# S5 states by two full-width sums and four transfers, gate banks read under priority, seven-product sums on VectorE, running column sum added last

## The chip, the cores and the metric

The kernel runs on one NeuronCore of a Trainium2 chip. Five engines work from queues of their own and wait for each other by semaphores: PE (TensorE, matmuls), DVE (VectorE), ACT (ScalarE), POOL (GpSimd) and SP (SyncE, which here only issues transfers). The time is the device time of one execution in microseconds, and lower is better. The time before is a median of 3 runs.

## The reference, cut to what matters

One inference step of a two-layer hybrid decoder over 1048 columns (16 meta tokens, 1024 prompt tokens, 8 sample tokens), all in float32. Layer 0 has a gated linear attention beside an S5 state space model; layer 1 is a Griffin block, a gelu branch times an RG-LRU recurrence; each layer ends with a gated feed-forward network.

```
# S5: a diagonal complex scan, then the output from the states
Ar, Ai, xr, xi = lax.associative_scan(_cplx_combine, (a_re, a_im, bu_re, bu_im), axis=1)
x0r = x0_re.astype(f32)[:, None]
x0i = x0_im.astype(f32)[:, None]
xr, xi = xr + Ar * x0r - Ai * x0i, xi + Ar * x0i + Ai * x0r
y = (jnp.einsum('ghp,btgp->btgh', c_re.astype(f32), xr)
     - jnp.einsum('ghp,btgp->btgh', c_im.astype(f32), xi)
     + d.astype(f32) * uf).reshape(B_, T, S5_W)
# rmsnorm, ahead of each mixer and each feed-forward network
y = xf * lax.rsqrt(jnp.mean(xf * xf, axis=-1, keepdims=True) + EPS)
```

## The kernel before

The model's width of 1024 lies on partitions in 8 tiles of 128, the columns on the free axis in chunks of 352, 352 and 344 (or 262 in layer 1). Every float32 product is three fp32r matmuls: an operand is split into a high part (`whi`, `H`, cast by ACT on line 85) and a low part (`wlo`, `L`, a subtraction on DVE), and `mm3` (lines 128 to 130) sums high times high, low times high and high times low in one PSUM bank. There are four such banks with the tag "bank" and four with the tag "aux", whose tiles are called `p`. A bank comes free when DVE or ACT has read it. The elementwise helpers `tt` (line 45) and `stt` (line 48) record most operations of DVE and POOL, so that tiles tell operations apart better than lines.

The stages by time in the trace: inputs to 60 us; the S5 states to 225; attention, GLU and output projection to 476; the rest of the output projection and the preparation of the first feed-forward to 541; feed-forward up to 968 and down to 1240; the RG-LRU layer to 1725; its last output projection and the preparation of the second feed-forward to 1784; feed-forward up to 2200 and down to the end.

**S5.** The 32 channel groups come in four states of 8. For one state, small tables are made on DVE, POOL and PE (`s5tm`, `s5CA`, `s5E`; PE transposes `s5E` on line 366), the inputs are projected (line 400), and `s5_states` rotates, scans (line 432) and rotates back, with `s5WC` and `s5WS` as the rotation, made by POOL. The parts of the rotation back are `s5ZA` and `s5VR`; their sum or difference is the state, `s5XP`, which is `[128, 8, 138]`: real and imaginary part on the two halves of the partitions, one column range for each group, while `s5ZA` and `s5VR` have two groups on the halves of the partitions. `s5XR` and `s5SO` are the small pieces for the sample columns and the output states. PE then forms the output by pairs, a matmul with `s5U` on line 465 and one with `s5XP` on line 466, and ACT evicts it. Between these pieces PE computes the products for K, Q and V.

**First feed-forward, preparation.** The feed-forward multiplies in a seven-product scheme (`Seven`). For each of four pairs of tiles, `Seven.sums` forms four differences `t` of gained halves, each then split to `T` by ACT and DVE. All this runs beside the output projection, whose banks DVE adds to the residual `X` under priority, and beside the running sum `acc` of squares on POOL.

**Griffin layer.** A step (half of the columns, group of three tiles) makes `rR` in xr, then the gelu branch in `gelu_branch` (six banks, each read by DVE as `rgg <- bank * RB`), then the recurrences on DVE (`rh`, `rig`, a scan on line 1540), the product of both (`rgg <- rgg * rh`, split to `ryh` and `ryl`), and the output projection. **After the last output projection** (`after`) come the squares for the norm: tiles 0 to 5 go into `acc` on POOL, which a matmul with ones (`colsum`, line 147) sums over the partitions into a bank `tot`; tiles 6 and 7 are summed straight into it.

The order on each engine is not written by hand. A scheduler takes the program's order, a model of readiness and the priorities given by `tc.high_priority()`, and fixes one order for each engine; waits come from the tiles that are shared.

Of the kernel before, what the change touches and what calls it, by code (L numbers as in the profile page):

```python
# [9 lines left out]
F32 = mybir.dt.float32  # L10
# [4 lines left out]
MUL, ADD, SUB = ALU.mult, ALU.add, ALU.subtract  # L15
# [24 lines left out]
def hybrid_step_kernel(ctx: ExitStack, tc: tile.TileContext, a: dict):  # L40
    nc = tc.nc
    V, A, P, PE = nc.vector, nc.scalar, nc.gpsimd, nc.tensor

    def tt(o, x, y, op, eng=None):
        return (eng or V).tensor_tensor(out=o, in0=x, in1=y, op=op)  # L45
# [13 lines left out]
    ps = ctx.enter_context(tc.tile_pool(name="ps", bufs=8, space=PSUM))  # L59
# [86 lines left out]
    def colsum(p, x, first=True, last=True):  # L146
        PE.matmul(out=p, lhsT=ones, rhs=x, start=first, stop=last)
# [25 lines left out]
    RB = qk.tile([128, T], F32, name="RB")  # L173
# [157 lines left out]
    NG, NI = 8, 4  # L331
# [50 lines left out]
    def s5_states(bi, d, tabs):  # L382
# [10 lines left out]
        VR = s5p.tile([128, 2, NI, 138], F32, name="s5VR")  # L393
        for j in range(0, NI, 2):
            m = 2
            for par in range(2):
                p = ps.tile([128, 2, 146], F32, name="p", tag="aux", bufs=4)
# [37 lines left out]
        XR = s5p.tile([128, 3, 2, NI, 8], F32, name="s5XR")  # L435
        nc.sync.dma_start(out=XR[:, 0], in_=a["s5xr"][:, :, sl])
        A1 = d["A1"]
        tt(XR[:, 1], XR[:, 0], A1[:, 0, sl].unsqueeze(1).unsqueeze(3).to_broadcast([128, 2, NI, 8]), MUL)
        tt(XR[:, 2, 0], XR[:, 0, 1], A1[:, 2, sl].unsqueeze(2).to_broadcast([128, NI, 8]), MUL)
        tt(XR[:, 2, 1], XR[:, 0, 0], A1[:, 1, sl].unsqueeze(2).to_broadcast([128, NI, 8]), MUL)  # L440
        tt(XR[:, 1], XR[:, 1], XR[:, 2], ADD)
        tt(SO[:, :, :, 0:8], XR[:, 1], VR[:, :, :, 0:8], ADD)
        tt(ZA, ZB, wc, MUL)
        tt(VC[:, 0], ZB[:, 1], WS, MUL)
        tt(VC[:, 1], ZB[:, 0], WS, MUL)
        XP = s5p.tile([128, NG, 138], F32, name="s5XP")
        P.memset(XP[:, :, 0:1], 0.0)
        nc.sync.dma_start(out=XP[:, :, 130:138], in_=a["s5xh"][:, g0:g0 + NG])
        for ri in range(2):
            for par in range(2):  # L450
                rows = slice(par * 64, par * 64 + 64)
                xo = XP[ri * 64:ri * 64 + 64].rearrange("p (i two) c -> p i two c", two=2)[:, :, par]
                tt(xo[:, :, 1:130], ZA[rows, ri, :, 0:129], VC[rows, ri, :, 0:129], ADD if ri else SUB)
            tt(SO[:, ri, :, 8], ZA[:, ri, :, 129], VC[:, ri, :, 129], ADD if ri else SUB)
        P.dma_start(out=a["o_s5"][:, :, sl], in_=SO)
        return U, XP

# [535 lines left out]
    class Seven(Stats):  # L993
# [18 lines left out]
        def sums(self, j, x1, x2, pool):  # L1012

            g1, g2 = (CV[:, self.gain + m:self.gain + m + 1] for m in (j, j + 4))
            b12, t1, t2 = (pool.tile([128, HALF], F32, name="t7", bufs=3) for _ in range(3))

            def gained(o, x, g):
                A.activation(out=o, in_=x, func=ACTF.Copy, scale=g)

            gained(t1, x1[:, :HALF], g1)  # L1020
            gained(b12, x1[:, HALF:], g1)
            tt(t1, b12, t1, SUB, P)
            gained(t2, x2[:, HALF:], g2)
            tt(b12, t2, b12, SUB, P)
            tt(t2, t2, t1, SUB, P)
            split(*self.o["T2", j], t2)
            split(*self.o["T3", j], b12)
            split(*self.o["T1", j], t1)
            gained(t1, x2[:, :HALF], g2)
            tt(t1, t1, t2, SUB, P)  # L1030
            split(*self.o["T4", j], t1)

        def gained(self, m, x):
# [521 lines left out]
    def gelu_branch(half, G, ws):  # L1555
        h0 = half * HALF
        ggs = []
        for w in ws:
            gg = rq.tile([128, HALF], F32, name="rgg", bufs=3)
            for c0, n in HCH:  # L1560
                p = bank()
                mm3(p[:, :n], kslices(w), cols(HL[half], c0, n))
                tt(gg[:, c0:c0 + n], p[:, :n], RB[:, h0 + c0:h0 + c0 + n], MUL)
            ggs.append(gg)
        return ggs

# [18 lines left out]
    def after(m, c0, n):  # L1585

        x = X[m][:, c0:c0 + n]
        if m in (0, 1, 4, 5):
            if m == 0:
                nxt.acc[c0] = tp.tile([128, 352], F32, name="acc", bufs=3)  # L1590
            sumsq_step(nxt.acc[c0], x, n, m == 0)
            if m == 5:
                tot[c0] = ps.tile([128, 512], F32, name="p", tag="aux", bufs=4)[:, :n]
                colsum(tot[c0], nxt.acc.pop(c0)[:, :n], last=False)
        else:

            q = tp.tile([128, 352], F32, name="sq", bufs=2)
            A.square(out=q[:, :n], in_=x)
            colsum(tot[c0], q[:, :n], first=False, last=m == 7)
            if m == 7:  # L1600
                A.activation(out=RB[:, c0:c0 + n], in_=tot[c0], func=ACTF.Sqrt, bias=eps, scale=1.0 / 1024)
                nxt.late.append((0, c0, n))
        if c0 + n == T:
            P.dma_start(out=xdn[m][:, HALF:], in_=X[m][:, HALF:])
            nxt.gained(m, X[m][:, HALF:])
            if m >= 4:
                g = nxt.sums_in(m - 4, X[m - 4], X[m])
                next(g)
                if m < 6:
                    next(g)  # L1610
                else:
                    rest.append(g)
# [196 lines left out]
```

## Time and profile before

| | |
|---|---|
| median of 3 runs | 2488.47 us (2487.82 to 2498.07) |
| profiled execution | 2490.02 us, of which the span is 2488.2 us |
| PE busy | 2372.1 us, 95% of the span |
| DVE busy | 1802.1 us, 72% |
| ACT, POOL busy | 1139.8 us, 589.9 us |
| mean granted TensorE clock | 0.978 of full speed |

The span runs from the first to the last instruction. PE is the engine to look at: what it does not fill of the span is idle, and a view of what ended each idle time names the engine that it waited for. The clock column (PEclk) is the share of the full 2.4 GHz that was granted; in this trace a stretch is either at 1.00 or at 0.50, so a mean between is a mix of both.

### The profile page before, as it was taken

The page shows a single profiled execution, that of the slowest core. Times are in us where ns is not written, and L with a number is a line of the kernel's source. Part 1 is how long each engine was busy: PE and PEld are TensorE (multiplying, and loading weights), DVE is VectorE, ACT ScalarE, POOL GpSimd, SP SyncE. Part 2 cuts the span into 40 slices and gives each one's busy share as a digit, 9 for nine tenths or more (in the row PEclk, how much of TensorE's full clock was granted, in tenths as well). Part 3 has the DMA queues.
Part 4 walks back from the last instruction along what each step waited for, and adds up shares of the span by engine and source line. Part 5 has one row for each costly group of instructions (what it writes and reads, how often), then busy time and mean ns, then how long its engine had stood idle before and what let it go on. Part 6 is the DMA issues. An engine that isn't in the chain of part 4 may idle for free.

```text
span 2488.2 us, 45222 instructions
## 1 busy us (share of the span) xinstructions
PE 2372.1 (95%) x17443; PEld 2326.2 (93%) x17443; DVE 1802.1 (72%) x3183; ACT 1139.8 (46%) x2302; POOL 589.9 (24%) x607
## 2 busy tenths in 40 slices
PE   6879999989999999999999999999799999999998
PEld 6768988879999999999999999998799999999997
DVE  9885788688777777554688777777877777766445
ACT  5224564554444444321576666665544444453123
POOL 4331000283443332000220002210333333310003
PEclk9999999989999999999999999999899999999999
DMA  3422225633333332632133333323333333336221
GB/s 117 108 70 80 87 71 168 212 128 122 118 116 116 116 116 94 211 109 89 43 90 94 99 99 122 93 89 100 128 116 116 116 116 116 116 119 195 90 82 70
DMA packets 200831, 277.09 MB, mean 111 GB/s; under 512 B 34440, under 2 KB 114264, under 8 KB 200616
## 3 DMA queue, kind: packets, MB, share of 16 engines
q1 hardware_dynamic: 191016, 261.94, 33.1%
q0 software_dynamic: 2848, 9.81, 1.0%
q10 hardware_dynamic: 6752, 2.45, 0.4%
q8 instruction: 137, 2.24, 0.4%
q14 instruction: 78, 0.64, 0.1%
HBM read 216.69 MB, written 51.43 MB: 108 GB/s over the span
## 4 chain that ended last, share of the span: by engine, by line
PE 74%; DVE 8%; issue 5%; DMA 3%; ACT 2%; POOL 1%; SPq 0%; DVEq 0%; POOLq 0%; ACTq 0%
PE bank L128 18%; PE bank L129 18%; PE bank L130 18%; PE p L128 6%; PE p L129 6%; PE p L130 6%; DVE X L45 1%; DVE wlo L45 1%; DVE rh L1540 1%; DMA hr<-hdr 1%; PE p L779 1%; DMA hr<-xdn 1%; DVE rig L48 0%; DMA SS<-in_st 0%; POOL acc L45 0%
## 5 line engine op out<-in xcount | busy, mean ns | idle before, releaser
L85 ACT CAST whi<-wraw 128x512 fp32r<-128x512 f32 (+2 forms) x449 | 262.1, 590 | 450.5 <-PE bank L129 328.0
L45 DVE TENSOR_TENSOR wlo<-wraw,whi 128x512 fp32r<-128x512 f32 (+2 forms) x448 | 327.9, 738 | 127.6 <-ACT whi L85 112.6
L45 DVE TENSOR_TENSOR X<-X,bank 128x352 f32<-128x352 f32 (+4 forms) x388 | 187.1, 486 | 194.8 <-PE bank L130 192.8
L128 PE MATMUL bank<-ph,whi 128*128 128x352 f32 (+1 forms) x912 | 293.1, 322 | 2.0 <-DVE X L45 1.8
L129 PE MATMUL bank<-pl,whi 128*128 128x352 f32 (+1 forms) x912 | 294.0, 322 | 0.0
L130 PE MATMUL bank<-ph,wlo 128*128 128x352 f32 (+1 forms) x912 | 293.7, 322 | 0.0
L45 POOL TENSOR_TENSOR acc<-acc,sq 128x352 f32<-128x352 f32 (+3 forms) x97 | 106.7, 1105 | 556.4 <-ACT sq L143 555.2
L85 ACT CAST whi<-wS 128x512 fp32r<-128x512 f32 x176 | 109.0, 620 | 262.2 <-PE p L129 127.1
L45 DVE TENSOR_TENSOR wlo<-wS,whi 128x512 fp32r<-128x512 f32 x176 | 125.2, 712 | 122.3 <-ACT whi L85 120.6
L128 PE MATMUL bank<-b,whi 128*128 128x262 f32 x560 | 164.2, 293 | 18.3 <-DVE rgg L45 9.8
L128 PE MATMUL bank<-H,whi 128*128 128x352 f32 (+1 forms) x480 | 161.4, 339 | 18.0 <-DVE X L45 8.1
L128 PEld LDWEIGHTS bank<-ph,whi 128*128 128x128 f32 x912 | 171.3, 188 | 3.2 <-DVE X L45 2.6
L129 PEld LDWEIGHTS bank<-pl,whi 128*128 128x128 f32 x912 | 171.3, 188 | 0.8
L130 PEld LDWEIGHTS bank<-ph,wlo 128*128 128x128 f32 x912 | 171.3, 188 | 0.0
L45 POOL TENSOR_TENSOR wS<-wA 128x512 f32<-128x512 f32 x88 | 151.5, 1721 | 69.5 <-DVE wlo L45 60.7
L129 PE MATMUL bank<-L,whi 128*128 128x352 f32 (+1 forms) x480 | 160.9, 337 | 7.0 <-DVE L L48 7.0
L130 PE MATMUL bank<-b,wlo 128*128 128x262 f32 x560 | 163.0, 291 | 3.9 <-DVE wlo L45 3.9
L129 PE MATMUL bank<-b,whi 128*128 128x262 f32 x560 | 163.1, 291 | 0.0
L128 PE MATMUL bank<-a,whi 128*128 128x262 f32 x560 | 160.5, 287 | 0.4 <-DVE rgg L45 0.4
L130 PE MATMUL bank<-H,wlo 128*128 128x352 f32 (+1 forms) x480 | 158.9, 333 | 1.7 <-DVE wlo L45 1.7
L129 PE MATMUL bank<-a,whi 128*128 128x262 f32 x560 | 159.9, 285 | 0.0
L130 PE MATMUL bank<-a,wlo 128*128 128x262 f32 x560 | 159.2, 284 | 0.0
(474 smaller groups left out, 7982.6 us busy)
## 6 DMA issues: line engine op xcount, KB each, us to landing
wA<-in_w_up SPq DMA_DIRECT2D x176, 256.0 KB, 2.7
wraw<-in_w_up SPq DMA_DIRECT2D x132, 256.0 KB, 4.8
wraw<-in_w_in SPq DMA_DIRECT2D x96, 256.0 KB, 2.8
hr<-hdr SPq DMA_DIRECT2D x44, 524.0 KB, 3.9
hdr<-VL SPq DMA_DIRECT2D x42, 524.0 KB, 4.0
wraw<-in_w_dn SPq DMA_DIRECT2D x80, 256.0 KB, 2.9
wraw<-in_w_out SPq DMA_DIRECT2D x48, 256.0 KB, 2.6
hr<-xdn SPq DMA_DIRECT2D x16, 524.0 KB, 3.6
```

The costliest lines, as they stand in the source:

```text
L45: return (eng or V).tensor_tensor(out=o, in0=x, in1=y, op=op)
L85: A.copy(out=h, in_=x)
L128: PE.matmul(out=out, lhsT=wh, rhs=xh, start=first and i == 0, stop=False, **kw)
L129: PE.matmul(out=out, lhsT=wh, rhs=xl, start=False, stop=False, **kw)
L130: PE.matmul(out=out, lhsT=wl, rhs=xh, start=False, stop=last and i == n - 1, **kw)
L779: PE.matmul(out=pas[c // 2][j0:j0 + m, c % 2, hp, :, j0 // 2:j0 // 2 + x], lhsT=lv[:, hp, c * C + j0:c * C + j0 + m], rhs=qz[:, :, hp, c * ...
L1540: V.tensor_tensor_scan(out=r[:, :npr], data0=av[:, :npr], data1=ig[:, :npr], initial=hprev[:, t:t + 1], op0=MUL, op1=ADD)
```

## The change

Four edits. In `s5_states` the five small operations on `XR` and `SO` go from DVE to POOL. The last combination, four half-width operations into `XP` and two small ones into `SO`, becomes two full-width operations on DVE into `ZB` (which is free by then), four transfers from `ZB` into `XP` (64 partitions, 4 groups, 129 columns: pieces of 516 bytes, 132 KB each; two issued by SP, two by ACT), and one copy for `SO` on POOL. In `Seven.sums` the four subtractions go from POOL to DVE. In `gelu_branch` the reads of the banks are put under `tc.high_priority()`. In `after`, for the last step, `tot` is allocated at tile 2 of the second half of tiles and not with the running sum, and the column sum of `acc` is added last, at tile 7.

```
-        tt(XR[:, 1], XR[:, 0], A1[:, 0, sl].unsqueeze(1).unsqueeze(3).to_broadcast([128, 2, NI, 8]), MUL)
...
-        tt(XR[:, 1], XR[:, 1], XR[:, 2], ADD)
-        tt(SO[:, :, :, 0:8], XR[:, 1], VR[:, :, :, 0:8], ADD)
+        tt(XR[:, 1], XR[:, 0], A1[:, 0, sl].unsqueeze(1).unsqueeze(3).to_broadcast([128, 2, NI, 8]), MUL, P)
...
+        tt(XR[:, 1], XR[:, 1], XR[:, 2], ADD, P)
+        tt(SO[:, :, :, 0:8], XR[:, 1], VR[:, :, :, 0:8], ADD, P)
...
         for ri in range(2):
+            tt(ZB[:, ri], ZA[:, ri], VC[:, ri], ADD if ri else SUB)
             for par in range(2):
-                rows = slice(par * 64, par * 64 + 64)
                 xo = XP[ri * 64:ri * 64 + 64].rearrange("p (i two) c -> p i two c", two=2)[:, :, par]
-                tt(xo[:, :, 1:130], ZA[rows, ri, :, 0:129], VC[rows, ri, :, 0:129], ADD if ri else SUB)
-            tt(SO[:, ri, :, 8], ZA[:, ri, :, 129], VC[:, ri, :, 129], ADD if ri else SUB)
+                (nc.sync if par else A).dma_start(out=xo[:, :, 1:130], in_=ZB[par * 64:par * 64 + 64, ri, :, 0:129])
+        P.tensor_copy(out=SO[:, :, :, 8], in_=ZB[:, :, :, 129])
         P.dma_start(out=a["o_s5"][:, :, sl], in_=SO)
...
-            tt(t1, b12, t1, SUB, P)
+            tt(t1, b12, t1, SUB)
             gained(t2, x2[:, HALF:], g2)
-            tt(b12, t2, b12, SUB, P)
-            tt(t2, t2, t1, SUB, P)
+            tt(b12, t2, b12, SUB)
+            tt(t2, t2, t1, SUB)
...
-            tt(t1, t1, t2, SUB, P)
+            tt(t1, t1, t2, SUB)
...
-                tt(gg[:, c0:c0 + n], p[:, :n], RB[:, h0 + c0:h0 + c0 + n], MUL)
+                with tc.high_priority():
+                    tt(gg[:, c0:c0 + n], p[:, :n], RB[:, h0 + c0:h0 + c0 + n], MUL)
...
-            if m == 5:
+        else:
+
+            if m == 2:
                 tot[c0] = ps.tile([128, 512], F32, name="p", tag="aux", bufs=4)[:, :n]
-                colsum(tot[c0], nxt.acc.pop(c0)[:, :n], last=False)
-        else:
-
             q = tp.tile([128, 352], F32, name="sq", bufs=2)
             A.square(out=q[:, :n], in_=x)
-            colsum(tot[c0], q[:, :n], first=False, last=m == 7)
+            colsum(tot[c0], q[:, :n], first=m == 2, last=False)
             if m == 7:
+                colsum(tot[c0], nxt.acc.pop(c0)[:, :n], first=False)
```

DVE at the first of the four states, from the last product of the rotation back (`s5VR`) to the sum `s5E` of the next table, before:

```order
247 L45 TENSOR_TENSOR s5VR<-s5ZB,s5WS 128x4x130
248 L45 TENSOR_TENSOR s5XP<-s5ZA,s5VR 64x4x129
249 L45 TENSOR_TENSOR K<-bank,RB 128x352
250 L45 TENSOR_TENSOR s5XP<-s5ZA,s5VR 64x4x129 x2
251 L45 TENSOR_TENSOR s5SO<-s5ZA,s5VR 128x4
252 L45 TENSOR_TENSOR s5XP<-s5ZA,s5VR 64x4x129
253 L45 TENSOR_TENSOR s5SO<-s5ZA,s5VR 128x4
254 L45 TENSOR_TENSOR s5XR<-s5XR,s5A_265 128x64
255 L45 TENSOR_TENSOR s5XR<-s5XR,s5A_265 128x32 x2
256 L45 TENSOR_TENSOR wlo<-wraw,whi 128x512
257 L45 TENSOR_TENSOR s5XR<-s5XR 128x64
```

and after:

```order
240 L45 TENSOR_TENSOR s5VR<-s5ZB,s5WS 128x4x130
241 L45 TENSOR_TENSOR wlo<-wraw,whi 128x512
242 L45 TENSOR_TENSOR K<-bank,RB 128x352
243 L45 TENSOR_TENSOR s5ZB<-s5ZA,s5VR 128x520 x2
244 L45 TENSOR_TENSOR wlo<-wraw,whi 128x512 x2
245 L45 TENSOR_TENSOR K<-bank,RB 128x344
246 L45 TENSOR_TENSOR wlo<-wraw,whi 128x512 x2
247 L45 TENSOR_TENSOR s5tm<-s5CB,s5P_260 128x576
248 L45 TENSOR_TENSOR s5KT<-s5KT,s5dd 16x4x16
249 L45 TENSOR_TENSOR s5CA<-s5CA,s5tm 128x576
```

The `s5XP`, `s5SO` and `s5XR` operations are gone from DVE's queue, and two sums into `s5ZB` stand in their place.

PE at the third state, from the last matmuls for V ahead of the output pairs to the first pair, before (the first row's two matmuls need only `s5U`; line 466 needs the state):

```order
654 L465 MATMUL p<-s5U,s5TT 128x138 x2
655 L129 MATMUL bank<-wlo,H_116 128x256
656 L130 MATMUL bank<-whi,L_117 128x256
657 L128 MATMUL bank<-whi,H_118 128x256
658 L129 MATMUL bank<-wlo,H_118 128x256
659 L130 MATMUL bank<-whi,L_119 128x256
660 L128 MATMUL bank<-whi,H_120 128x256
661 L129 MATMUL bank<-wlo,H_120 128x256
662 L466 MATMUL p<-s5XP,s5CA 128x138
```

and after, the end of the same stretch:

```order
693 L130 MATMUL bank<-whi,L_129 128x256
694 L128 MATMUL bank<-whi,H_114 128x256
695 L129 MATMUL bank<-wlo,H_114 128x256
696 L130 MATMUL bank<-whi,L_115 128x256
697 L128 MATMUL bank<-whi,H_116 128x256
698 L129 MATMUL bank<-wlo,H_116 128x256
699 L130 MATMUL bank<-whi,L_117 128x256
700 L467 MATMUL p<-s5XP,s5CA 128x138
```

More matmuls for V stand ahead of the first use of the state: counted in these orders from the projection of the state's inputs (line 400) on, 68 before and 89 after; for the second state 69 and 82, for the first 132 and 126.

DVE at one step of the Griffin layer, the recurrences of the three tiles, before:

```order
1843 L45 TENSOR_TENSOR rh<-rh,rig 128x8
1844 L1540 SCALAR_TENSOR_TENSOR rh<-ra,hprev,rig 128x516
1845 L45 TENSOR_TENSOR wlo<-wraw,whi 128x512
1846 L1547 COPY hout<-rh 128x9
1847 L45 TENSOR_TENSOR rh<-ra,H_13998 128x8
1848 L45 TENSOR_TENSOR rgg<-bank,RB 128x262
1849 L45 TENSOR_TENSOR rh<-rh,rig 128x8
1850 L45 TENSOR_TENSOR rgg<-bank,RB 128x262
1851 L1547 COPY hout<-rh 128x9
1852 L45 TENSOR_TENSOR rgg<-bank,RB 128x262
1853 L45 TENSOR_TENSOR rgg<-rgg,rh 128x524
```

and after:

```order
1837 L45 TENSOR_TENSOR rgg<-bank,RB 128x262
1838 L45 TENSOR_TENSOR rh<-rh,rig 128x8
1839 L48 SCALAR_TENSOR_TENSOR rig<-rig,rh 128x524
1840 L1548 COPY hout<-rh 128x9
1841 L48 SCALAR_TENSOR_TENSOR rh<-ra,rh 128x524
1842 L1541 SCALAR_TENSOR_TENSOR rh<-ra,hprev,rig 128x516
1843 L45 TENSOR_TENSOR wlo<-wraw,whi 128x512
1844 L45 TENSOR_TENSOR rgg<-bank,RB 128x262
1845 L45 TENSOR_TENSOR rh<-ra,H_14002 128x8
1846 L48 SCALAR_TENSOR_TENSOR rig<-rig,rh 128x524
1847 L45 TENSOR_TENSOR wlo<-wraw,whi 128x512
1848 L45 TENSOR_TENSOR rh<-rh,rig 128x8
```

The three reads `rgg<-bank`, which stood together behind the last scan, now stand between the recurrences (the first of the three is six rows above this piece).

## Rows read from the trace of the kernel before

**Rows 1.** The profile's page: the busy time of the engines and their share of the span.

```profile
PE 2372.1 (95%) x17443; PEld 2326.2 (93%) x17443; DVE 1802.1 (72%) x3183; ACT 1139.8 (46%) x2302; POOL 589.9 (24%) x607
```

**Rows 2.** Busy time by stage: the stretch in us from the start and its length, then busy us (and instructions) of each engine, the granted clock, the DMA share and GB/s.

```profile
60.00:200.00 140.00, 112.73 (x698) 104.89 (x697) 119.64 (x244) 33.53 (x78) 49.77 (x53) 0.90 0.35 88
...
476.00:541.00 65.00, 52.47 (x284) 49.54 (x285) 52.63 (x60) 39.92 (x74) 49.94 (x48) 0.87 0.43 149
541.00:968.00 427.00, 427.00 (x3495) 426.42 (x3494) 314.25 (x440) 184.17 (x358) 172.69 (x153) 1.00 0.34 114
```

**Rows 3.** What PE waited for from 60 to 200 us: us in total, how often, the longest.

```profile
PE p L366 <- DVE s5E L45: 15.4, 6, 4.6
PE p L466 <- issue: 5.8, 2, 2.9
PE p L466 <- DVE s5XP L45: 5.0, 2, 4.7
```

**Rows 4.** PE's timeline at these waits: start, us, instruction, and in brackets the idle time before it.

```profile
116.43 0.83 PE L466 MATMUL p<-s5XP,s5CA 128*128 128x138 f32 x2 [4.69 <-DVE s5XP L45]
...
132.05 1.09 PE L366 MATMUL p<-ID,s5E 128*128 128x128 f32 x4 [4.64 <-DVE s5E L45]
...
160.49 0.63 PE L366 MATMUL p<-ID,s5E 128*128 128x128 f32 x4 [4.23 <-DVE s5E L45]
...
193.57 0.63 PE L366 MATMUL p<-ID,s5E 128*128 128x128 f32 x4 [1.42 <-DVE s5E L45]
```

**Rows 5.** DVE's operations from 60 to 200 us by form: count, busy us, mean ns.

```profile
L45 DVE TENSOR_TENSOR s5XP<-s5ZA,s5VR 64x516 f32<-64x516 f32 x12 | 11.0, 913 | 0.2
L45 DVE TENSOR_TENSOR s5XR<-s5XR,s5A 128x64 f32<-128x64 f32 x4 | 10.8, 2711 | 0.0
...
L45 DVE TENSOR_TENSOR s5ZB<-s5VR,s5WS 128x520 f32<-128x520 f32 x6 | 4.2, 695 | 4.4 <-ACT s5VR L402 4.4
```

**Rows 6.** The timeline at the first state: DVE, then POOL (its four operations in a row, the first two of them in one row).

```profile
112.68 0.69 DVE L45 TENSOR_TENSOR s5VR<-s5ZB,s5WS 128x520 f32<-128x520 f32 x1
...
119.04 5.00 DVE L45 TENSOR_TENSOR s5XR<-s5XR 128x64 f32<-128x64 f32 x1
...
119.28 2.18 POOL L45 TENSOR_TENSOR s5ZA<-s5WB,s5WK 128x520 f32<-128x520 f32 x2
...
122.64 1.31 POOL L45 TENSOR_TENSOR s5WS<-s5WS,s5ZA 128x520 f32<-128x520 f32 x1
```

**Rows 7.** Transfers issued up to 240 us: count, KB each, median us from issue to landing; and the stretch of SP's queue in which it issues those of `s5TT`.

```profile
s5U<-us SPq DMA_DIRECT2D x4, 520.0 KB, 5.4
...
vdr<-vo SPq DMA_DIRECT2D x8, 128.0 KB, 1.7
...
129.73 14.11 SPq L378 DMA_DIRECT2D s5TT<-s5KT  x16
```

**Rows 8.** What PE waited for from 476 to 541 us.

```profile
PE bank L128 <- DVE X L45: 8.1, 6, 2.1
PE p L147 <- POOL acc L45: 4.4, 1, 4.4
```

**Rows 9.** Operations of DVE and then of POOL from 476 to 541 us by form: count, busy us, mean ns; and the spread of one of them (least, median, longest ns).

```profile
L48 DVE SCALAR_TENSOR_TENSOR B<-X,CV,B 128x524 fp32r<-128x524 f32 x11 | 17.6, 1599 | 2.5 <-ACT B L89 2.2
L45 DVE TENSOR_TENSOR T<-t,T 128x524 fp32r<-128x524 f32 x12 | 15.2, 1278 | 4.1 <-ACT T L85 3.8
...
L45 POOL TENSOR_TENSOR t<-t,t 128x524 f32<-128x524 f32 x14 | 19.1, 1366 | 4.9 <-ACT t L1018 4.3 <-issue 0.4
L45 POOL TENSOR_TENSOR acc<-acc,sq 128x352 f32<-128x352 f32 x14 | 16.6, 1186 | 0.8 <-ACT sq L143 0.8
...
L45 DVE TENSOR_TENSOR T<-t,T x12: 692/1342/2033, 483.8 to 532.6; 128x524 fp32r<-128x524 f32 x12
```

**Rows 10.** The timeline in one pair of that stretch: DVE, where one such operation elsewhere takes 0.75 us (first row) and here 3.95, and POOL beside it.

```profile
505.03 0.75 DVE L48 SCALAR_TENSOR_TENSOR B<-X,CV,B 128x524 fp32r<-128x524 f32 x1
...
508.08 3.95 DVE L48 SCALAR_TENSOR_TENSOR B<-X,CV,B 128x524 fp32r<-128x524 f32 x1 [0.84 <-ACT B L89]
...
507.99 1.32 POOL L45 TENSOR_TENSOR t<-t,t 128x524 f32<-128x524 f32 x1
...
510.18 1.28 POOL L45 TENSOR_TENSOR t<-t,t 128x524 f32<-128x524 f32 x1
```

**Rows 11.** The gate branch: what PE waited for from 1520 to 1680 us; the first matmul after the third of these waits, and the first of `out` (with `ryh`) in that step; the splits that `out` needs, with the starts of the first and the last; and the first and the last of the three stretches at half clock behind these waits (start and length, busy us of PE, its weight loads, DVE, ACT and POOL, granted clock).

```profile
PE bank L128 <- DVE rgg L45: 9.4, 3, 3.5
...
1660.78 0.59 PE L128 MATMUL bank<-b,whi 128*128 128x262 f32 x1 [2.96 <-DVE rgg L45]
...
1678.20 0.28 PE L128 MATMUL bank<-ryh,whi 128*128 128x262 f32 x1
...
L45 DVE TENSOR_TENSOR ryl<-rgg,ryh x9: 687/697/701, 1537.4 to 1670.0; 128x524 fp32r<-128x524 f32 x9
...
1533.73:1537.14 3.41, 3.41 (x17) 3.41 (x17) 3.06 (x8) 3.05 (x6) 0.00 (x0) 0.50 0.26 77
...
1660.02:1666.85 6.83, 6.07 (x28) 6.07 (x29) 5.44 (x16) 3.44 (x6) 0.00 (x0) 0.50 0.20 58
```

**Rows 12.** After the last output projection: what PE waited for from 1725 to 1784 us, and the busy times of 20 us in it.

```profile
PE p L147 <- POOL acc L45: 2.7, 1, 2.7
...
1745.00:1765.00 20.00, 20.00 (x154) 19.41 (x152) 19.86 (x31) 17.15 (x35) 6.07 (x8) 1.00 0.36 120
```

## What I predict, and why

> **What bounds the kernel now.** I read the page first, then busy times by stage, then PE's waits stage by stage. PE is busy for 95% of the span [rows 1], so the stages differ: feed-forward up is full (427.00 of 427 us) and can gain nothing, while from 60 to 200 us PE fills 112.73 of 140 us and from 476 to 541 only 52.47 of 65 [rows 2]. The reader is to see in the same rows the granted clock: 0.90 and 0.87 there, 1.00 in the full stage. A stretch at 0.50 comes right behind a wait of PE: PE starts again at 1660.78 after 2.96 us idle, and the stretch from 1660.02 to 1666.85 is at 0.50, which is 1.2 of 2.4 GHz [rows 11]. So a wait is paid twice, as idle time and as half-speed matmuls after it. Over 140 us a mean of 0.90 means 28 us at half clock, up to 14 us lost.
>
> Since the stages that follow are PE-full, what a wait of PE loses ahead of them shifts all later work, and what it gives back comes through to the end. The sum therefore goes by PE's waits that each edit touches, and by the clock behind them. It is made against the profiled execution, 2490.0 us (span 2488.2); the median is 1.5 us lower.
>
> **Edit 1, the S5 states.** From 60 to 200 us PE waits 15.4 us for `s5E` and 10.8 us for `s5XP` (5.0, and 5.8 put down to issue at the same instruction) [rows 3].
>
> What it removes. An `XR` operation took 5.00 us at 119.04, while POOL ran its four operations from 119.28 to 123.95 in a row [rows 6]; four operations of one such form take 10.8 us together, 2711 ns on average, for 64 elements per partition [rows 5]. On DVE they stand ahead of the sums that make the next table. PE then waits for `s5E` at three places behind such a stall: 4.64, 4.23 and 1.42 us, 10.3 in all [rows 4]. With `XR` on POOL that stall can't stand there; but `s5E` needs POOL's product as well, which is queued behind POOL's four operations, and the `SO` copy now waits for `ZB` at the head of them. From the end of `s5VR` (112.68 + 0.69 = 113.4), about 2.5 us for both `ZB` sums and a weight split between, 4.7 us for the four (119.28 to 123.95), and some 3 more for the tables put the next `s5E` near 125, and PE would arrive near 123. I leave 4 of the 10.3 us standing and take 6 away. Bounds: 0 and 10.3.
>
> What it adds. The state now comes from two sums of 0.695 us [rows 5], 1.4 us, and then transfers. Before, the first matmul with the state ran 3.1 us after the end of `s5VR` (116.43 less 113.37) [rows 4, 6], with `s5XP` operations of 913 ns [rows 5]. No row shows these four transfers of 132 KB in 516-byte pieces. The nearest are 128 KB in 1.7 us, and 520 KB in 520-byte pieces, as much as all four together, in 5.4 us [rows 7]. Two queues issue them and they run side by side, so I take 3.0, between them; the state is then ready 4.4 us after `s5VR`, 1.3 later than now, and between 0 and 3.7 later at the ends. In the changed order 13 more matmuls stand ahead of the second state's first use and 21 more ahead of the third's, 2.1 and 2.5 us at 0.16 and 0.12 us each, while the first has 6 fewer, 1 us. So three states: 3 x 1.3 + 1 - 4.6, about 0 (from -4 to +7). The last state has over 100 matmuls ahead of it and no wait now.
>
> A page of the Trainium skill prices such a transfer: "DMA: Bandwidth & Descriptors", section "Anatomy of one DMA — SWDGE (gpsimd) path", gives about 2.0 us fixed plus bytes at 436 GB/s; an estimate by it is 2.3 us each, 0.7 us under my value, with which the sum would be 2 us lower. The 128 KB row at 1.7 lies under that rule, the 520 KB row at 5.4 above its 3.2.
>
> DVE also sheds work: 11.0 us of `s5XP` for 5.6 of sums, and the `XR` group; of its 119.64 us in 140 [rows 2] some 20. That makes every later table and bank read earlier, and is the cover for the later state. A third of PE's idle gone should give back about a third of the up to 14 us of clock; I take 4. Sum of edit 1: -10, from +7 to -18 (10.3 + 4 of waits, 4 of clock).
>
> **Edit 2, the sums of the first feed-forward.** From 476 to 541 PE waits 8.1 us for `X` and 4.4 for `acc` at the end [rows 8]. `X` is DVE's read of a bank, under priority, so it is late because the operation in front is slow: a `B` that takes 0.75 us takes 3.95 while POOL runs `t`, `acc`, `t` from 507.99 to 511.46 [rows 10]. The excess is 11 x (1.60 - 0.75) + 12 x (1.28 - 0.69), 16 us on DVE [rows 9, 10]. The edit adds 16 x 0.69, 11 us, to DVE and takes 16 x 1.37, 22 us, from POOL, which is busy for 49.94 of 65 us [rows 2, 9] and feeds the last `acc`. If half of the excess goes with half of POOL's work, DVE gains 8 and pays 11 over the four pairs, 3 us more; but the chain ACT, POOL, ACT, DVE of each difference loses a hop to the queue that POOL's `acc` operations stand in, and `X` no longer waits 3.95. I take half of the two waits, 6 us, and 1 of clock: -7. Ends: -12 (both waits), and for a DVE that becomes the bound: it now works 13.2 us a quarter of the stage (52.63 of 65 us [rows 2], stalls included); four differences at 0.69 make 15.9, under the 16.25 that a quarter lasts, but stalled as the median `T` is, 1.34 [rows 9], they make 18.5, 2.3 us too much in each quarter: +9.
>
> The row shows DVE held up for as long as POOL's run lasts. The Trainium skill, "SBUF — State Buffer", section "Who interferes with whom", says that a VectorE operation with two SBUF inputs and a GpSimd operation that reads SBUF exclude each other, for the whole instruction, and that the order of issue decides who blocks. By that rule the differences on DVE hold the pair too, for 0.69 in place of 1.37 us: an estimate of 16 x 0.68, 11 us, off the sum of holding times, and -9 for the edit where I take -7. Its "whole instruction" is shorter than what the trace has: there DVE waited through three of POOL's.
>
> **Edit 3, the gate branch.** PE waits 9.4 us for three reads `rgg` of banks that were long full [rows 11]; DVE had them behind the recurrences. In the new order they stand between the recurrences, two to six operations sooner, over 2.9 us ahead at each place. The work of DVE is the same, so the end of the recurrence stays where it is. Behind each wait lies a stretch at half clock: 3.41 us, another such, and 6.83 with 6.07 busy [rows 11]; half of the busy time is lost, 6.4. What is late next? `out` needs `ryl`: the last is split by 1670.0 + 0.7 = 1670.7; `out` starts at 1678.20, and would without the 2.96 us and 2.8 of clock at 1672.4, 1.7 us of margin [rows 11]. So the waits go whole: -15, from -16 to -8 (half comes back at `ryl` or at the next bank).
>
> **Edit 4, the running sum.** A wait of 2.7 us for `acc` goes [rows 12]. But soon after DVE is busy for 19.86 of 20 us [rows 12] and carries the splits on which PE ends up waiting; a free wait there moves into the next. -0.5, from -2.7 to 0.
>
> **Sum.** -10 - 7 - 15 - 0.5 = -32.5: 2457.5 against the profiled execution, 2456 against the median.
>
> **Rivals.**
> - A, *the transfers eat the S5 gain*. They land like the 520 KB row, 5.4 us, or SP holds them up a little, and the `s5E` waits turn into waits for the state: edit 1 is 0 or +2, time 2466 to 2468. For it: the pieces are as small as in that row. Against it: two queues, less in each.
> - B, *DVE becomes the bound* from 476 to 541: stalls undiminished, the new differences among them, 18.5 us a quarter, +9 in place of -7: 2472. For it: DVE is busy 52.63 of 65 and pays 11 us. Against it: POOL loses two fifths of what stalls it.
> - C, *the gate waits come back* as waits for `ryl` or later bank reads; half of edit 3 is lost: 2464. For it: only 1.7 us of margin in the third step.
> - D, *slower*. SP's queue issues 16 transfers of `s5TT` in 14.11 us [rows 7]; were the `s5XP` transfers caught behind them in each state, the state would be some 10 us later, in four states, with ACT's evictions behind its own two transfers that wait. Forty us more, less the 4 of cover in the third and second, turns -32.5 into about +3.5: 2492, and more with the clock. It decides from a landing 8 us later than I take, 11 us after the sums. Against it: in the new order they stand ahead of the next state's sixteen.
> - E, *it does not do what it says*: the orders show that all four edits took effect, so no chance is left for it beyond the combinations below.
>
> **How the numbers follow.** Forecast (2445 to 2463) 0.52; A 0.14; C 0.11; B 0.10; better than all of it (both edits 1 and 2 near their best ends, 2438 to 2445) 0.05; A and B together, about 2484, 0.04; D 0.04. The range has to leave out 0.2 at most: 2438 to 2474 leaves out D and A with B, and what spills over. Half a per cent, 12.4 us, is about what a measurement of this kernel can tell from no change; faster means below 2476. Faster 0.87, same 0.08, slower 0.05.
>
> **What would show it.** Right: from 60 to 200 us no DVE operation of 64 elements over 1 us; the wait for `s5E` down from 15.4 to under 9; the wait at the matmul with `s5XP` between 7 and 15; the transfers landing in 2 to 4 us. From 476 to 541 the stage ends some 6 us sooner, with `B` under 1.3 us on average. No wait for `rgg` over 0.5 us and no stretch at half clock behind one. Wrong: `s5XP` waits of 20 us or more (A, D), PE waiting over 10 us for `X` or for splits (B), a wait for `ryl` or `ryh` of 2 us or more (C). What I trust least are the transfers, which no row shows.

## The result, and the profile after

The changed kernel takes 2469.46 us (median of 4 runs, 2466.97 to 2472.72) against 2490.64 us for the kernel before (4 runs). The ratio is 0.9917, with a 95% interval of 0.9903 to 0.9932: 21 us or 0.8% faster. The prediction was 2456 us with a range of 2438 to 2474; the time lies inside, near the slow end, and outside the band of 2445 to 2463 that had the chance of 0.52. Of the 32.5 us forecast, 23.0 came by the profiled executions (2490.02 to 2466.97).

Where they came from is read off PE's timeline, at instructions that both kernels share and that wait for the same thing. After (start, us, instruction, idle time before it), the first two and the last three of them:

```profile
474.05 0.95 PE L128 MATMUL bank<-H,whi 128*128 128x344 f32 x2 [1.88 <-ACT H L85]
...
525.91 1.54 PE L147 MATMUL p<-acc,ones 128*128 128x352 f32 x2 [3.48 <-POOL acc L45]
...
1300.82 0.39 PE L128 MATMUL bank<-ryh,whi 128*128 128x262 f32 x1 [0.35 <-DVE X L45]
...
1701.75 0.80 PE L128 MATMUL bank<-ryh,whi 128*128 128x262 f32 x4 [3.90 <-ACT ryh L85]
...
1750.67 0.59 PE L128 MATMUL bank<-b,whi 128*128 128x262 f32 x1 [8.35 <-ACT whi L85]
```

Before, the same instructions:

```profile
475.88 0.95 PE L128 MATMUL bank<-H,whi 128*128 128x344 f32 x2 [1.87 <-ACT H L85]
...
536.20 1.54 PE L147 MATMUL p<-acc,ones 128*128 128x352 f32 x2 [4.41 <-POOL acc L45]
...
1311.37 0.39 PE L128 MATMUL bank<-ryh,whi 128*128 128x262 f32 x1 [1.03 <-DVE X L45]
...
1724.38 0.86 PE L128 MATMUL bank<-ryh,whi 128*128 128x262 f32 x4 [3.89 <-ACT ryh L85]
...
1773.57 0.58 PE L128 MATMUL bank<-b,whi 128*128 128x262 f32 x1 [8.51 <-ACT whi L85]
```

Up to the first line the changed kernel has gained 1.8 us (475.88 - 474.05), which is what edit 1 left; at the second it is 10.3, so edit 2 gave 8.5; 10.6 at the third; at the fourth 22.6, so edit 3 gave 12.1; at the fifth 22.9, so edit 4 gave 0.3; and at the end 23.0. The terms had been 10, 7, 15 and 0.5. Edit 1 is the one that failed.

How far a single profile can be trusted in this is seen from the other kernels of the study, which share these instructions. Those with the S5 code of before reach the first line at 475.88, 476.51 (edit 1 undone), 477.37 (edit 3 alone) and 477.86 (edit 2 alone), those with the S5 code of after at 474.05, 474.18 (edit 1 alone) and 478.26 (edit 4 undone): the 1.8 us of edit 1 are not clear of that spread. Edits 2 and 3 are. From the first line to the second it takes 60.3 to 60.5 us in the three profiles without edit 2 and 51.9 to 52.6 in the eleven with it; from the second to the fourth 1186.9 to 1188.4 us in the three without edit 3 and 1174.5 to 1177.1 in the eleven with it.

Its waits after, from 60 to 225 us (us in total, how often, the longest; the state is read on line 467 now; the third row is the same wait for the fourth state, put down to another transfer that landed last):

```profile
PE p L467 <- DMA s5XP<-s5ZB: 15.1, 3, 6.1
PE p L366 <- DVE s5E L45: 6.2, 4, 4.8
PE p L467 <- DMA wraw<-in_w0f: 3.3, 1, 3.3
```

The wait for `s5E` fell from 15.4 to 6.2 us [rows 3], more than I had forecast, and VectorE shed 18 us in the stage (119.64 to 101.17 of 140 us). But the wait for the states rose from 10.8 to 18.4. Together they were 26.2 and are 24.6. Busy times by stage after, in the columns of [rows 2]:

```profile
60.00:200.00 140.00, 115.71 (x748) 109.04 (x748) 101.17 (x213) 35.11 (x80) 63.03 (x71) 0.91 0.40 101
476.00:541.00 65.00, 58.24 (x358) 55.85 (x357) 61.42 (x81) 42.97 (x81) 36.22 (x37) 0.94 0.44 155
...
1510.00:1660.00 150.00, 146.34 (x1189) 145.03 (x1188) 127.57 (x249) 99.14 (x181) 28.34 (x39) 1.00 0.30 91
```

The last row shows edit 3: a stretch with all three places in it and no half-clock piece, where [rows 11] had 3.41, 3.41 and 6.83 us at 0.50. What PE still waits for there, from 1500 to 1700 us, is the next bank:

```profile
PE bank L128 <- DVE rR L45: 3.6, 3, 1.6
```

In the preparation of the first feed-forward, VectorE's operations by form after (count, busy us, mean ns), from 473 to 527 us, answer to [rows 9]:

```profile
L45 DVE TENSOR_TENSOR t<-t,t 128x524 f32<-128x524 f32 x13 | 15.0, 1157 | 0.4 <-ACT t L1019 0.4
L48 DVE SCALAR_TENSOR_TENSOR B<-X,CV,B 128x524 fp32r<-128x524 f32 x10 | 11.8, 1183 | 0.1
L45 DVE TENSOR_TENSOR T<-t,T 128x524 fp32r<-128x524 f32 x12 | 10.1, 865 | 0.3 <-ACT T L85 0.3
```

`B` fell from 1599 to 1183 ns and `T` from 1278 to 865; the differences, now on VectorE, take 1157 and not 690. PE's waits there, from 476 to 541 us, against [rows 8]:

```profile
PE p L147 <- POOL acc L45: 3.5, 1, 3.5
PE bank L128 <- DVE X L45: 3.3, 5, 0.9
```

### The profile page after: what moved, and what is told of

Same layout as the page of the kernel before. It is cut to its first block, busy times and chain, and to the rows that moved or that the text cites. A ratio compares the mean times of both kernels' runs of the same rounds, so it can differ in the third digit from the quotient of the medians.

```text
span 2465.2 us, 45246 instructions
## 1 busy us (share of the span) xinstructions
PE 2362.5 (96%) x17443; PEld 2318.5 (94%) x17443; DVE 1776.8 (72%) x3163; ACT 1137.5 (46%) x2302; POOL 575.7 (23%) x615
## 4 chain that ended last, share of the span: by engine, by line
PE 75%; DVE 12%; issue 6%; DMA 3%; ACT 2%; POOL 1%; SPq 0%; ACTq 0%; DVEq 0%; POOLq 0%
PE bank L128 18%; PE bank L129 18%; PE bank L130 18%; PE p L128 6%; PE p L129 6%; PE p L130 6%; DVE wlo L45 1%; DVE X L45 1%; DVE L L48 1%; PE p L780 1%; DMA hr<-xdn 1%; DMA s5XP<-s5ZB 1%; PE p L467 1%; DVE s5ZA L45 1%; DMA hr<-hdr 0%
## 5 line engine op out<-in xcount | busy, mean ns | idle before, releaser
L45 POOL TENSOR_TENSOR acc<-acc,sq 128x352 f32<-128x352 f32 (+3 forms) x97 | 97.8, 1011 | 579.0 <-ACT sq L143 578.0
L128 PE MATMUL bank<-b,whi 128*128 128x262 f32 x560 | 161.1, 288 | 8.3 <-ACT whi L85 8.3
L129 PE MATMUL bank<-b,whi 128*128 128x262 f32 x560 | 160.5, 287 | 0.0
```

The costliest lines, as they stand in the source:

```text
L128: PE.matmul(out=out, lhsT=wh, rhs=xh, start=first and i == 0, stop=False, **kw)
L129: PE.matmul(out=out, lhsT=wh, rhs=xl, start=False, stop=False, **kw)
```

## The experiments

Times are medians; "before" was run beside each group on the same chip (2491.05, 2492.36 and 2491.04 us). The question was where edit 1's 10 us had gone, and whether edits 2 to 4 carry the gain by themselves.

**Edit 1 undone, the rest kept.** `s5_states` as before, edits 2 to 4 as in the change.

> The changed kernel with edit 1 undone, edits 2 to 4 kept. Theory T: edit 1 as it stands is worth only some 2 us (state ready 7 us after the last product of the rotation instead of 3, and the input norm held up on GpSimd, against shorter waits for the tables), so 2469 to 2473 and edits 2 to 4 give nearly the whole gain. Rival R: edit 1 gives the forecast 10 us and it is edits 2 and 3 that gave less than their waits: 2477 to 2480. In either case PE's wait for s5E should be back at about 15 us and the first of the norm's column sums should wait about 3.8 us instead of 6.0.

Measured: 2472.13 us, ratio 0.9921 (0.9905 to 0.9936). The `s5E` waits are back at 14.7 us, those for the states at 11.7. That is the changed kernel's 0.9917 within the intervals: edit 1 as it stands is worth 3 us by the medians, and by the intervals perhaps nothing.

**Edit 1 alone.** The other way round, on the kernel before.

> The kernel before with edit 1 alone. Theory Z: edit 1 trades waits, the sum of PE's waits for s5E and for the states stays near 25 us and the input norm is 2 us later, so the time is within 4 us of the kernel before, 2486 to 2493. Rival P, the prediction: 10 us faster, 2478 to 2483.

Measured: 2489.06 us, ratio 0.9992 (0.998 to 1.0005). P is out, and the two waits come to 25.1 us, as Z had it.

**Edits 2 and 3 alone**, each on the kernel before.

```
-            tt(t1, b12, t1, SUB, P)
+            tt(t1, b12, t1, SUB)
...
-                tt(gg[:, c0:c0 + n], p[:, :n], RB[:, h0 + c0:h0 + c0 + n], MUL)
+                with tc.high_priority():
+                    tt(gg[:, c0:c0 + n], p[:, :n], RB[:, h0 + c0:h0 + c0 + n], MUL)
```

> The kernel before with edit 3 alone. Theory T: the waits for rgg (9.4 and 0.8 us) and the half-clock stretches behind them (13.7 us) go, and 3.6 us of waits for rR come in their place: 12 to 13 us faster than before, 2476 to 2480. Rival R: the gain hangs on the earlier stages (the phase of the weight splits), and alone it is under 8 us: 2483 or above.

> The kernel before with edit 2 alone. Theory T: the stage from 476 to 541 us loses 8 us (waits for X from 8.1 to about 3.3, for acc from 4.4 to 3.5, half-clock stretches from 17.1 to 10.2 us): 2480 to 2484. Rival R: VectorE is held up as long as before with four more operations a pair, and the stage is no shorter: 2488 to 2493.

Measured: 2479.17 us for the gate branch, ratio 0.9956 (0.994 to 0.9972), 11 us; and 2481.16 for the sums, 0.9961 (0.9947 to 0.9975), 10 us. The gate kernel shows the same 3.6 us of waits for `rR`, the sums kernel waits of 2.8 us for `X` and 3.5 for `acc`. The three ratios of single edits add up: 0.0008 + 0.0044 + 0.0039 is 0.0091, against 0.0083 for all.

**Edit 4 undone, the rest kept.**

> The changed kernel with edit 4 undone. Theory T: the wait at the column sum was only exchanged for another (2.7 us for acc, 2.5 us for the square), so the time is that of the changed kernel within 1 us, 2468 to 2471. Rival R: the gain is real and was hidden by the spread, 2472 to 2474.

Measured: 2470.5 us, 0.9914 (0.9896 to 0.9932). PE waits 2.7 us for `acc` there, 2.5 us for a square in the changed kernel. The wait was exchanged, as T had it.

**The two halves of edit 1 apart.** First the states on VectorE again, `XR` on GpSimd:

```
-            tt(ZB[:, ri], ZA[:, ri], VC[:, ri], ADD if ri else SUB)
...
-                (nc.sync if par else A).dma_start(out=xo[:, :, 1:130], in_=ZB[par * 64:par * 64 + 64, ri, :, 0:129])
+                tt(xo[:, :, 1:130], ZA[rows, ri, :, 0:129], VC[rows, ri, :, 0:129], ADD if ri else SUB)
```

> The changed kernel with the states written by DVE in four half-width operations as before, instead of through ZB and four transfers; the small XR operations stay on GpSimd. Theory T: the transfers are what eats edit 1; the first matmul with a state runs 3 to 4 us after the last product again, the waits for the states fall from 18.4 us to 8 to 11, the waits for s5E stay near 6 to 8: 2459 to 2464. Rival R: the 11 us of half-width operations on DVE come back as later tables, s5E waits 10 us or more, and the time stays at 2467 to 2471.

Measured: 2479.66 us, 0.9954 (0.994 to 0.9967), 10 us slower than the changed kernel and outside both expectations. The waits for the states did fall to 11.5 us, nearly as T said (8 to 11), but those for `s5E` rose to 18.0. Taking the transfers away was no gain at all, and T as I had put it fell. VectorE's timeline at the first state shows what happened to the stall:

```profile
119.28 0.69 DVE L45 TENSOR_TENSOR s5XP<-s5ZA,s5VR 64x516 f32<-64x516 f32 x1
120.00 0.17 DVE L45 TENSOR_TENSOR s5SO<-s5ZA,s5VR 128x4 f32<-128x4 f32 x1
120.08 6.40 DVE L45 TENSOR_TENSOR wlo<-wraw,whi 128x512 fp32r<-128x512 f32 x2
```

There is no `XR` on VectorE any more, and two weight splits of 0.68 us each take 6.40. GpSimd's run of four lies at 121.27 to 125.93 here, and the second split ends 0.6 us behind it. The stall that [rows 6] shows on `XR` has found another operation.

So the second theory (T2): the stall belongs to GpSimd's run, not to `XR`. The other half tests it, the states by transfers and `XR` on VectorE:

> The other half of edit 1 alone (edits 2 to 4 kept): the states go through ZB and the four transfers, the small XR and SO operations stay on VectorE. Theory T2: what shortened PE's wait for s5E is that the half-width operations left VectorE; who pays for GpSimd's run of four is whichever two-input operation stands beside it, so XR's place is worth nothing there and costs 2 us ahead of the input norm. Then s5E waits stay at 5 to 9 us with XR on VectorE, one operation beside the run still takes about 5 us, and the time is 2460 to 2468, not above the changed kernel. Rival P, the prediction's own step: the stalled XR is what s5E waits for, so its waits come back to 12 us or more and the time is 2473 to 2480.

Measured: 2471.74 us, 0.9917 (0.9902 to 0.9932), the changed kernel's ratio to the last digit; its absolute time is 4 us over what T2 gave and 1 us under what P gave. The `s5E` waits are 7.4 us although `XR` is back on VectorE and one of its operations takes 3.04 us again; the waits for the states are 17.4:

```profile
PE p L467 <- DMA s5XP<-s5ZB: 12.7, 2, 8.1
PE p L366 <- DVE s5E L45: 7.4, 5, 4.3
PE p L467 <- DMA s5BB<-in_s5b: 4.7, 1, 4.7
```

P is out by the waits: where `XR` stands does not decide those for `s5E`.

**Without `XR`.** The sharpest form: edit 1 undone, and the small operations left out (the sample columns of the S5 output states are set to zero).

```
-        tt(XR[:, 1], XR[:, 0], A1[:, 0, sl].unsqueeze(1).unsqueeze(3).to_broadcast([128, 2, NI, 8]), MUL)
...
-        tt(SO[:, :, :, 0:8], XR[:, 1], VR[:, :, :, 0:8], ADD)
+        P.memset(SO[:, :, :, 0:8], 0.0)
```

> The changed kernel with edit 1 undone and with the five small XR and SO operations of each state left out altogether (their part of the output states is set to zero). It is to be set against e1_no_s5, which has them on VectorE. Theory T2: a five-microsecond stall of VectorE beside GpSimd's run of four stays, on another operation (a weight split or a table product), the waits for s5E stay at 11 us or more, and the time is that of e1_no_s5 within 3 us, 2469 to 2474. Rival P, the prediction's step: the stall belongs to XR, the s5E waits fall to 9 us or less, 2461 to 2466.

Measured: 2478.39 us (2475.76 to 2480.66), 6 us slower than the same kernel with the operations in it (2472.13, 2468.48 to 2473.8). Less work, more time. The stall stayed on another operation, as T2 had it; the time that T2 gave is missed. VectorE, then GpSimd beside it (its run of four is 121.55 to 126.21, 0.80 us of issue ahead of it):

```profile
120.37 6.40 DVE L45 TENSOR_TENSOR wlo<-wraw,whi 128x512 fp32r<-128x512 f32 x2
...
121.55 2.18 POOL L45 TENSOR_TENSOR s5ZA<-s5WB,s5WK 128x520 f32<-128x520 f32 x2
123.65 1.32 POOL L45 TENSOR_TENSOR s5WC<-s5WC,s5ZA 128x520 f32<-128x520 f32 x1
124.90 1.31 POOL L45 TENSOR_TENSOR s5WS<-s5WS,s5ZA 128x520 f32<-128x520 f32 x1
```

and PE waits longer for `s5E` than in any other kernel of this study:

```profile
PE p L366 <- DVE s5E L45: 20.1, 4, 6.2
```

Why it is the slower one stays open. Of its 6 us, 2.7 are there before this stall: PE's first projection of a state's inputs (line 400) starts at 90.56 us, with the operations in it at 87.88.

**The first state's small operations on VectorE, the others on GpSimd**, alone and with the states on VectorE.

```
+        xeng = V if bi == 0 else P
-        tt(XR[:, 1], XR[:, 1], XR[:, 2], ADD, P)
+        tt(XR[:, 1], XR[:, 1], XR[:, 2], ADD, xeng)
```

> The changed kernel with the five small operations of the first state alone back on DVE. Theory T: on GpSimd they wait for the start tables in front of the running sum of the input norm; with them away the wait of the norm's column sum falls from 6.0 to about 3.8 us and the clock behind it recovers (10.2 us at half clock before 60 us now, 3.4 before the change): 2464 to 2467. Rival R: the sum of squares is late by itself (ScalarE's squares), and nothing moves: 2468 to 2471.

> Both: states written by DVE, the first state's small operations on DVE, those of the other three on GpSimd. Theory T: the two add up, 2454 to 2460, and this beats the changed kernel. Rival R: each only moves a wait, and the pair stays at 2465 or above.

Measured: 2471.42 us (2463.61 to 2476.32) and 2475.73 (2470.43 to 2477.55). The mechanism ahead of the first state was right: in the changed kernel GpSimd waits for start tables with `XR` in its queue ahead of `acc`, PE's wait at the input norm is 6.0 us, and 3.8 with the first state's `XR` moved away. PE then waits 8.3 us at the first state, not 6.1, and even so stays ahead: its projection for the fourth state starts at 196.29, in the changed kernel at 200.32. But nothing of it was left at the first line of the anchors, 476.49 against 474.05. It went in the attention stage between, where from 200 to 300 us the granted clock is 0.93 in the one and 0.98 in the other; why stays open. With the states on VectorE the move came through (2479.66 to 2475.73). In that kernel the stall at the first state is on three weight splits, 7.00 us, and the projection for the second state starts at 133.90, as with the stall on `XR` (134.18, edit 1 undone): moving the stall cost nothing there. T fell for the pair, which beats the kernel before but not the changed one.

**How much the landing costs.** Two ways of changing when the state is ready: one half of it written by VectorE while the other is transferred, and eight transfers of 66 KB.

> The changed kernel with the imaginary half of each state going first through ZB and its two transfers, while VectorE writes the real half itself with two half-width operations. The state is ready 2 to 3 us sooner than in the changed kernel, and VectorE has one operation more in each state. Theory Z (the two waits trade): the waits for the states fall by 6 us or more, those for s5E rise by 4 or more, time 2466 to 2472. Rival L (landing is a pure cost): only the first happens, 2458 to 2464.

> The changed kernel with each of the four transfers of a state cut in two (eight of 66 KB): two more issues of some 0.65 us on each queue. Theory L: the last issue is the price, the state is 1 to 1.5 us later in each of four states and the time 2473 to 2476. Rival Z: the later state is paid back by shorter s5E waits, 2468 to 2472. A landing that does not get later at all would say that the transfers are bound by bytes, not by issue.

Measured: 2470.97 us and 2468.87, ratios 0.9914 (0.9896 to 0.9932) and 0.9907 (0.9889 to 0.9926). In the first the waits for the states fall by 5.2 us (18.4 to 13.2) and those for `s5E` rise by 4.9 (6.2 to 11.1): Z, but for the size of the first. In the second the transfers do not get later, they land sooner, so L's premise was wrong. Its transfers (count, KB each, median us from issue to landing) and its waits:

```profile
s5XP<-s5ZB SPq DMA_DIRECT2D x16, 64.5 KB, 2.2
s5XP<-s5ZB ACTq DMA_DIRECT2D x16, 64.5 KB, 2.5
```

```profile
PE p L468 <- DMA s5XP<-s5ZB: 12.5, 4, 5.0
PE p L366 <- DVE s5E L45: 9.7, 4, 5.4
```

Again 5.9 us less at the states and 3.5 more at `s5E`, and the same time as the changed kernel within the intervals. The trade is not all of it: both kernels reach the projection for the fourth state 1.9 us sooner than the changed one (198.45 and 198.35 against 200.32) and stand level with it at the first anchor (474.48 and 473.70 against 474.05). No kernel here beats it beyond them.

## Why the prediction was right, and which step failed

**The way and the range were right**, and for edits 2 and 3 so was the reason: PE-full stages pass on what the waits before them give back. The gain of 10.3 us ahead of the first feed-forward is 10.6 behind it, and the 22.9 ahead of the second are 23.0 at the end. For edit 1 the premise did not hold: the stage behind it, from 200 to 474 us, is not full (PE fills 256.74 of 274 us), and what kernels above had won by 200 us was gone at its end. The range held because it also covered rival A; the forecast itself was 13 us too fast.

**Edit 1, -10 forecast, 0 to -3 measured: the steps that failed are "I leave 4 of the 10.3 us standing and take 6 away", which took the stall to be `XR`'s, and the term of the states, "about 0 (from -4 to +7)", which measured +7.6 (10.8 to 18.4 us): +4.3 at the first three, and 3.3 at the fourth, for which I had no wait.** One sign that I had named, `s5E` waits under 9 us, came true at 6.2 without the gain; the other, 7 to 15 us for the states, did not.
- *The cause of the `s5E` wait.* I took the 5.00 us row of `XR` for a slow operation whose removal would remove the stall. But the stall is not its own, and whatever stands next in VectorE's queue pays: two weight splits take 6.40 us when `XR` is elsewhere or not there at all. That much is shown by the kernels above. That GpSimd's run of four causes it is read from the times, since the stalled operation ends right behind the run (124.04 behind 123.95 before, 126.48 behind 125.93 and 126.77 behind 126.21 with the splits); no kernel took the run away. Nor did `s5E` come "near 125", a sum that by its own terms (113.4 + 2.5 + 4.7 + 3) is 123.6: it ends at 132.76, before at 131.91.
- *The state's readiness.* I had it 4.4 us after the end of `s5VR`. In the changed kernel `s5VR` ends at 115.3 and the first matmul with the state runs at 122.53, 7.2 us later. VectorE's rows and the landings, over all sixteen transfers:

```profile
114.64 0.69 DVE L45 TENSOR_TENSOR s5VR<-s5ZB,s5WS 128x520 f32<-128x520 f32 x1
115.25 0.68 DVE L45 TENSOR_TENSOR wlo<-wraw,whi 128x512 fp32r<-128x512 f32 x1
115.85 0.52 DVE L45 TENSOR_TENSOR K<-bank,RB 128x352 f32<-128x352 f32 x1
116.28 2.67 DVE L45 TENSOR_TENSOR s5ZB<-s5ZA,s5VR 128x520 f32<-128x520 f32 x2
```

```profile
DMA to landing us min/median/max: 2.7/3.4/4.8
```

One us of other work stands ahead of the sums, the sums take 2.67 us and not 1.4, and the last of the four lands about 3.6 us after them (118.95 to 122.53). My 3.0 for the landing was near the median of 3.4; a state needs the last. At the second and third state the way from the end of `s5VR` to the first matmul is 7.9 and 6.6 us, before 3.5 and 3.1, so that each of the three came some 4 us later and not 1.3. The Trainium skill's price for such a landing ("DMA: Bandwidth & Descriptors", "Anatomy of one DMA — SWDGE (gpsimd) path"), an estimate of 2.3 us, is below every one of these sixteen landings; that section is about transfers that GpSimd issues, and these were issued by SP and ACT.

- *The input norm*, for which I had no term. `XR` on GpSimd holds up the running sum there, and the S5 stage starts later. PE's projections of the inputs (line 400) for the first and second state, before and then after:

```profile
86.80 3.64 PE L400 MATMUL p<-s5U,s5G 128*128 128x138 f32 x16
134.89 3.49 PE L400 MATMUL p<-s5U,s5G 128*128 128x138 f32 x16
...
90.53 2.48 PE L400 MATMUL p<-s5U,s5G 128*128 128x138 f32 x16
134.44 2.15 PE L400 MATMUL p<-s5U,s5G 128*128 128x138 f32 x16
```

The first state did get shorter, from 48.1 to 43.9 us, but 3.7 had been lost ahead of it (with the first state's `XR` on VectorE the first projection is at 87.42; the other kernels with the S5 code of before have it between 87.75 and 89.11, so that 1.4 to 3.7 us are edit 1's). The second and third state take as long as before, 34.1 us both times, and 31.8 against 31.3.

Why a later state is paid back at `s5E`, and an earlier one is not, can be read in the same traces. After, PE does the first transposes and products of the next table behind the state's matmuls, and VectorE waits for what comes of them (first PE, line 370; then VectorE, whose `s5E` is in the same queue):

```profile
122.53 0.83 PE L467 MATMUL p<-s5XP,s5CA 128*128 128x138 f32 x2 [6.11 <-DMA s5XP<-s5ZB]
...
127.52 1.05 PE L370 MATMUL p<-s5CA,s5E 128*16 128x128 f32 x8
132.91 0.63 PE L366 MATMUL p<-ID,s5E 128*128 128x128 f32 x4 [0.30 <-DVE s5E L45]
...
129.28 0.87 DVE L45 TENSOR_TENSOR s5KT<-s5KT,s5dd 16x64 f32<-16x64 f32 x1 [2.75 <-ACT s5KT L372]
```

The second transposes ran at 132.05 before [rows 4] and run at 132.91 now. By the clock of the span `s5E` did not become earlier. PE came to it later, since the stage had begun later and PE had stood 6.11 us at the state; of the wait of 4.64 us 0.30 is left. What VectorE shed it now spends waiting for that product of PE (`s5KT`), from 60 to 225 us before and after:

```profile
DVE s5KT L45 <- ACT s5KT L372: 3.0, 2, 2.4
...
DVE s5KT L45 <- ACT s5KT L372: 21.6, 4, 10.8
```

The kernels in which VectorE writes the states wait 3.0 to 8.1 us there, those with transfers 8.3 to 22.5. PE's two waits together lie between 21.6 and 31.1 us in the kernels of the study, and the three with 29 and more are the slowest of those that have edits 2 to 4. That one common chain (state, matmuls, transposes, table, next state) is the bound of the stage is my reading of these rows; no kernel took the chain itself apart.

**Edit 2, -7 forecast, -8.5 in the profile and -10 alone.** The step "If half of the excess goes" holds: `B` lost 416 of an excess of some 850 ns, `T` 413 of some 590. The wait for `X` fell by 4.8 us, more than half; that for `acc` by 0.9. The clock gave more than the 1 us that I took: from 474.00 to 536.20 before and from 473.00 to 526.00 after, with 265 matmuls in both, PE's busy time fell from 47.80 to 45.19 us and the mean clock rose from 0.90 to 0.96. The new differences are stalled too, 1157 ns, close to the median `T` that I gave for the bad end, and still VectorE was not the bound: rival B's price was near, its conclusion was wrong.

**Edit 3, -15 forecast, -12.1 and -11 alone.** The term was mis-sized by "so the waits go whole". The waits for `rgg` and the half-clock stretches went whole; 3.6 us of waits for `rR` came in their place, three times at the first matmul of `out` (0.85, 1.63 and 1.09 us, the clock at 1.00 throughout). That is the second clause of rival C, "or later bank reads", at half of what C took back (7.5 us). 9.4 + 6.4 - 3.6 is 12.2.

**Edit 4, -0.5 forecast, -0.3.** As worked out.

**The rivals.** A came nearest: its time was 2466 to 2468, and its mechanism, `s5E` waits turning into waits for the state, is what the rows show, at a landing of 3.4 and not 5.4. I gave it 0.14. D did not happen: the landings never came near 11 us.

## What to carry to other kernels

An operation that took 5 us for 64 elements was not slow here, it was waiting; before moving such a one, ask which operation stands behind it in the queue, since that one may wait next, as it did here. Two waits of one engine that belong to one loop of work can't be added up as two savings: sum them in the trial as in the original, and if the sum stays, the edit moved a wait. Reads that free a bank are worth pulling ahead of long work on the same engine, and a wait can cost more than its length: the three here, of 3 us or so each, took half-clock stretches with them when they went, while the shorter waits that came in their place, 1.63 us at most, had none behind them.

## What the runs showed that I had not expected

Leaving out twenty small VectorE operations made the kernel 6 us slower (2472.13 to 2478.39); the stall then fell on two weight splits, but what made it slower is not known. Cutting each transfer in two made the landings shorter, 2.2 and 2.5 us for 64.5 KB against 2.8 and 3.5 for 129 KB, although each queue issued twice as many:

```profile
s5XP<-s5ZB SPq DMA_DIRECT2D x8, 129.0 KB, 2.8
s5XP<-s5ZB ACTq DMA_DIRECT2D x8, 129.0 KB, 3.5
```

And the stall can fall on the other engine: in the changed kernel one product of GpSimd (`s5WC`; 1.11, 2.09 and 1.10 us at the other three states) took 5.18 us while VectorE ran without a gap from 180.66 to 185.05.

```profile
180.82 5.18 POOL L45 TENSOR_TENSOR s5WC<-s5WB,s5WK 128x520 f32<-128x520 f32 x1 [7.75 <-DVE s5ZA L45]
```
